# Transposing the residual and the spatial weights on VectorE instead of TensorE in a two-layer decoder trunk

## Chip, cores and metric

The kernel runs on one core of a Trainium2 chip. The metric is the device time of one execution in microseconds; the time of the kernel before is the median of three runs. The profile is of one execution, and times in it count from the start of its span.

## What is computed

A trunk of two layers over 256 positions of width 2048, all in float32. The parts that the change touches are the spatial gate of layer 0 and the residual on its way to the output:

```python
# layer 0: 12 heads g, chunks of 128 positions
w = w_sp * jnp.tril(jnp.ones((CHUNK, CHUNK), w_sp.dtype))
sv = jnp.einsum('gts,bnsgc->bntgc', w, vb) + b_sp.T[None, None, :, :, None]
...
# end of layer 1
x = x + jnp.concatenate([main, mo], axis=-1) @ w_out[l]
x = x + conv_ffn(rmsnorm(x, g_ffn[l]), w_ffn_up[l], conv_w[l], conv_b[l], w_ffn_down[l])
return rmsnorm(x, g_final)
```

The product with `w_sp` sums over s, so TensorE needs each head's 128x128 matrix with s on the partitions, that is, transposed. The residual `x` is kept with features on the partitions (`self.x`, called xT in the profile: 16 blocks of 128 features x 256 positions). The last matrix product and the final norm work with positions on the partitions, so `x` is transposed once into `xt` (two blocks of 128 positions x 2048).

## The kernel before

Nearly all of the work is products of a streamed weight with an activation. Every operand is split in two parts, hi and lo, and each product is made of three matmuls (hi by hi, hi by lo, lo by hi). A weight is read in chunks of 512 KB: `chunk` (L97 on) has SyncE issue the transfer into `raw` (L103; four buffers), ScalarE write the hi part `whi` (L113; four buffers), VectorE write the lo part `wlo` (L114; five buffers), and then TensorE does the chunk's matmuls: `gemm_fm` with the weight as the stationary operand (L152, L153, L155), `gemm_tm` with the activation as the stationary operand (L184 to L186). A product with K = 2048 and 512 output columns is 8 chunks. The engines run as a chain of rings: `raw` of chunk n+4 can be loaded once VectorE has split chunk n, and `whi` of chunk n+4 can be written once TensorE has finished chunk n.

Small tasks are hung between chunks by tables of hooks: `hooks={2: [f]}` runs f in program order after chunk 2. A scheduler then places each instruction in its engine's own order; in places the program order is forced. All of the weight transfers, and the two groups of transfers below, are in the one queue of SyncE, and an engine and that queue each work strictly in order.

The spatial weights: in layer 0, after chunk 5 of the first of three products (`zhooks`, L768), `spatial_load` loads the bias `b_sp` (L755) and `w_sp` (L758, one transfer, tile wsp). During the third product `spatial_turn` (L760) runs after chunks 2, 3 and 4: four TensorE transposes into one PSUM tile (L763), then a VectorE multiplication by the triangular mask `keep` that writes the transposed weights (L765, into the tile slots). They are used some 25 us later. In the same stretch the rotary angles are computed by short VectorE instructions (L350 to L376).

The residual: in layer 1's feed-forward part, the second up-projection of the second group of columns has the hooks `turns` (L1165): after chunks 4 to 7 it runs `turn` (L1110) twice each. A `turn` is four TensorE transposes of 128x128 (L1115) into PSUM and one ScalarE copy to `xt` (L1116). `xt` is first read by `tokens` about 100 us later.

Of the kernel before, what the change touches and what calls it, by code (L numbers as in the profile page):

```python
# [12 lines left out]
AF = mybir.ActivationFunctionType  # L13
ALU = mybir.AluOpType
AX = mybir.AxisListType

P = 128
D = 2048
S = 256
NB = D // P  # L20
GH = 12
GW = GH * 128
# [47 lines left out]
class Kernel:  # L70
# [666 lines left out]
    def layer_a(self):  # L737
        nc, t, tc = self.nc, self.t, self.tc
# [3 lines left out]
        with ExitStack() as ctx:  # L742
# [7 lines left out]
            wT, bb = (wb[:, i * GW : (i + 1) * GW].rearrange("p (g s) -> p g s", g=GH) for i in range(2))  # L750
            spatial = {}


            def spatial_load():
                nc.sync.dma_start(out=bb, in_=t["b_sp"][0].rearrange("(o g) t -> o g t", o=1).to_broadcast([P, GH, P]))  # L755
                raw = self.ap.tile([P, NB * 512], F32, tag="big", name=self.uid("wsp"))
                spatial["raw"] = raw[:, :GW].rearrange("p (g s) -> p g s", g=GH)
                nc.sync.dma_start(out=spatial["raw"], in_=t["w_sp"][0].rearrange("g t s -> t g s"))  # L758

            def spatial_turn(g):  # L760
                acc = self.psum()
                for i in range(4):
                    nc.tensor.transpose(acc[:, i * P : (i + 1) * P], spatial["raw"][:, g + i, :], self.ident)  # L763
                k3 = self.keep.rearrange("p (g s) -> p g s", g=1).to_broadcast([P, 4, P])
                nc.vector.tensor_tensor(wT[:, g : g + 4, :], acc.rearrange("p (g s) -> p g s", g=4), k3, ALU.mult)  # L765

            turns = {2 + i: [lambda i=i: spatial_turn(4 * i)] for i in range(3)}
            zhooks = ({2: [lambda: self.rope_angles(la)], 5: [spatial_load]}, {4: [self.rope_tables]}, turns)  # L768
            for c in range(3):
# [33 lines left out]
            p, parts = {}, {}  # L803
# [287 lines left out]
    def run(self):  # L1091
        nc, tc, t = self.nc, self.tc, self.t
        self.constants()
        with tc.tile_pool(name="mk", bufs=1) as self.mk:
            self.start()
            self.layer_a()
        self.ffn(0, lambda j: self.next_operand(j, None))
        self.layer_b()
        with tc.tile_pool(name="fin", bufs=1) as fin:

            xt = fin.tile([P, 2, D], F32, name="xt")
            gb = fin.tile([P, D], F32, name="gb")
            sums = fin.tile([P, 2, 5], F32, name="fsums")
            part = fin.tile([P, 2], F32, name="fpart")
            r = fin.tile([P, 2], F32, name="froot")
            q = fin.tile([P, 2], F32, name="fq")
            v = fin.tile([P, 2], F32, name="fv")
            nc.sync.dma_start(out=gb, in_=t["g_final"].rearrange("(o d) -> o d", o=1).to_broadcast([P, D]))

            def turn(j):  # L1110
                acc = self.psum()
                for tb in range(2):
                    for i in range(2):
                        o = (2 * tb + i) * P
                        nc.tensor.transpose(acc[:, o : o + P], self.x[:, j + i, tb * P : (tb + 1) * P], self.ident)  # L1115
                nc.scalar.activation(xt[:, :, j * P : (j + 2) * P], acc.rearrange("p (a c) -> p a c", a=2), AF.Copy)  # L1116


            def tokens(j, tb, acc, last, half=None):
                c0, n = (0, 512) if half is None else (256 * half, 256)  # L1120
                c = slice(j * 512 + c0, j * 512 + c0 + n)
                o = xt[:, tb, c]
                add = lambda o, a: nc.vector.tensor_tensor(o, a, o, ALU.add)
                add(o, acc[:, c0 : c0 + n])
                if not last:
                    return
                junk = self.tmp(fin, [P, 512], "fjunk", 2)
                one = lambda x: x[:, tb : tb + 1]
                if half == 1:

                    nc.vector.tensor_tensor_reduce(
                        out=junk[:, :n], in0=o, in1=o, scale=-0.5 / D, scalar=one(part), op0=ALU.mult, op1=ALU.add, accum_out=one(v)
                    )
                else:
                    nc.scalar.activation(junk[:, :n], o, AF.Square, accum_out=sums[:, tb, j : j + 1])
                if half == 0:
                    add(xt[:, tb, j * 512 + 256 : (j + 1) * 512], acc[:, 256:])
                if j < 3:
                    nc.vector.tensor_tensor(o, o, gb[:, c], ALU.mult)
                if j == 2:  # L1140

                    nc.vector.tensor_reduce(one(part), sums[:, tb, 0:3], AX.X, ALU.add)
                    nc.vector.tensor_scalar(one(part), one(part), -0.5 / D, -0.5 * EPS, ALU.mult, ALU.add)
                    nc.scalar.activation(one(r), one(part), AF.Sqrt, scale=-2.0)
                if j == 3:
                    if half != 1:
                        total = one(part) if half == 0 else one(v)
                        nc.vector.tensor_scalar(total, sums[:, tb, 3:4], -0.5 / D, one(part), ALU.mult, ALU.add)
                    if half == 0:
                        return  # L1150

                    nc.scalar.activation(one(r), one(v), AF.Sqrt, scale=-2.0)
                    nc.vector.reciprocal(one(r), one(r))
                    nc.vector.scalar_tensor_tensor(one(q), one(r), one(r), one(v), ALU.mult, ALU.mult)
                    nc.vector.scalar_tensor_tensor(one(r), one(q), 1.5, one(r), ALU.add, ALU.mult)

                    y, rows = xt[:, tb, :], slice(tb * P, (tb + 1) * P)
                    for a in (0, 1024):
                        nc.scalar.activation(y[:, a : a + 512], y[:, a : a + 512], AF.Copy, scale=one(r))
                    nc.vector.tensor_scalar(y[:, 512:1024], y[:, 512:1024], one(r), None, ALU.mult)  # L1160
                    nc.vector.scalar_tensor_tensor(y[:, 1536:], y[:, 1536:], one(r), gb[:, 1536:], ALU.mult, ALU.mult)
                    nc.sync.dma_start(out=self.out[0, rows, :1024], in_=y[:, :1024])
                    (nc.scalar if tb else nc.sync).dma_start(out=self.out[0, rows, 1024:], in_=y[:, 1024:])

            turns = {4: [lambda: turn(0), lambda: turn(2)], 5: [lambda: turn(4), lambda: turn(6)],  # L1165
                     6: [lambda: turn(8), lambda: turn(10)], 7: [lambda: turn(12), lambda: turn(14)]}
            self.ffn(1, to_tokens=turns, tokens=tokens)


# [24 lines left out]
```

## Time and profile before

| | us |
|---|---|
| median of 3 runs (lowest to highest) | 2059.01 (2058.97 to 2060.08) |
| time of the profiled execution | 2058.79 |
| its span | 2057.0 |
| TensorE busy | 2046.9 |
| VectorE busy | 1396.0 |
| ScalarE busy | 1085.6 |
| mean busy share of the DMA engines in most slices | 0.5 to 0.6 |

The busy times are sums over instructions; matmuls overlap, so a busy TensorE is read together with the distance between the starts of its instructions. In a row of the timeline stand the start, the duration, the engine, the line and operation, output and inputs, and in brackets the idle time before it with what ended that. PE is TensorE, DVE VectorE, ACT ScalarE, POOL GpSimd, SPq the DMA queue of SyncE.

### The profile page before, as it was taken

The numbers are of one execution on the slowest core, as the hardware profiler recorded it, in microseconds if no ns is written. First come the engines' busy times: TensorE is split into PE (matmuls) and PEld (weight loads), VectorE is DVE, ScalarE is ACT, GpSimd is POOL, SyncE is SP. The second block draws the span as 40 slices with busy tenths as digits, with TensorE's granted clock in tenths as the row PEclk, the third lists the DMA queues.
The fourth block names the chain that finished last, engine by engine and source line by source line (L and its number), as shares of the span: only waits on it lengthen the run. The fifth ranks groups of instructions, "written<-read, shape, count | busy, mean of one in ns | idle before, by whom it ended". The sixth has DMA issues, their size and how long they took to land.

```text
span 2057.0 us, 39914 instructions
## 1 busy us (share of the span) xinstructions
PE 2046.9 (100%) x16348; PEld 1979.9 (96%) x16348; DVE 1396.0 (68%) x2113; ACT 1085.6 (53%) x1588; POOL 142.0 (7%) x200
## 2 busy tenths in 40 slices
PE   9999999999999999999999999999999999999998
PEld 8989999999999999999999999999988999889996
DVE  6656766777656766457788786776765667646765
ACT  7754744555434555345555575455544555435554
POOL 0000013100000000000043241300000000000000
PEclk9999999999999999999999999999999999999999
DMA  8565555566556665566655635565655666556654
GB/s 288 188 217 176 160 193 198 190 195 195 195 195 195 193 193 193 194 193 194 195 195 176 187 118 178 187 204 177 193 193 194 196 195 195 187 193 195 197 181 154
DMA packets 207692, 392.58 MB, mean 191 GB/s; under 512 B 14158, under 2 KB 23188, under 8 KB 207380
## 3 DMA queue, kind: packets, MB, share of 16 engines
q1 hardware_dynamic: 207316, 389.48, 58.5%
q8 instruction: 128, 2.10, 0.4%
q10 hardware_dynamic: 192, 0.54, 0.1%
q14 instruction: 56, 0.46, 0.1%
HBM read 387.88 MB, written 2.10 MB: 190 GB/s over the span
## 4 chain that ended last, share of the span: by engine, by line
PE 99%; ACT 0%; DVE 0%; DMA 0%; issue 0%; ACTq 0%
PE ps L152 26%; PE ps L153 26%; PE ps L155 26%; PE ps L185 6%; PE ps L184 6%; PE ps L186 6%; PE ps L507 1%; PE ps L400 0%; PE ps L583 0%; PE ps L584 0%; PE ps L582 0%; PE ps L1001 0%; PE ps L790 0%; PE ps L1115 0%; PE ps L1029 0%; DMA graw<-in_g_mem 0%
## 5 line engine op out<-in xcount | busy, mean ns | idle before, releaser
L114 DVE TENSOR_TENSOR wlo<-raw,whi 128x1024 fp32r<-128x1024 f32 x660 | 818.4, 1243 | 531.1 <-ACT whi L113 525.0
L113 ACT ACTIVATE whi<-raw 128x1024 fp32r<-128x1024 f32 x660 | 700.6, 1062 | 857.8 <-PE ps L153 632.3
L152 PE MATMUL ps<-xhl,whi 128*128 128x256 f32 x3264 | 763.2, 277 | 0.0
L153 PE MATMUL ps<-xhl,whi 128*128 128x256 f32 x3264 | 761.2, 276 | 0.0
L153 PEld LDWEIGHTS ps<-xhl,whi 128*128 128x128 f32 x3264 | 612.9, 188 | 0.3
L152 PEld LDWEIGHTS ps<-xhl,whi 128*128 128x128 f32 x3264 | 612.7, 188 | 0.3
L155 PE MATMUL ps<-xhl,wlo 128*128 128x256 f32 x3264 | 436.7, 276 | 0.0
L155 PEld LDWEIGHTS ps<-xhl,wlo 128*128 128x128 f32 x3264 | 400.5, 188 | 0.0
L152 PE MATMUL ps<-h,whi 128*128 128x256 f32 x704 | 163.6, 276 | 0.0
L153 PE MATMUL ps<-h,whi 128*128 128x256 f32 x704 | 163.6, 276 | 0.0
L185 PE MATMUL ps<-wlo,h 128*128 128x512 f32 x354 | 137.2, 388 | 0.0
L184 PE MATMUL ps<-whi,h 128*128 128x512 f32 x354 | 136.8, 388 | 0.0
L186 PE MATMUL ps<-whi,h 128*128 128x512 f32 x354 | 136.8, 388 | 0.0
L153 PEld LDWEIGHTS ps<-h,whi 128*128 128x128 f32 x704 | 132.0, 188 | 0.0
L152 PEld LDWEIGHTS ps<-h,whi 128*128 128x128 f32 x704 | 131.8, 188 | 0.0
L152 PE MATMUL ps<-mainhl,whi 128*128 128x256 f32 x512 | 119.6, 277 | 0.0
L153 PE MATMUL ps<-mainhl,whi 128*128 128x256 f32 x512 | 119.3, 276 | 0.0
L694 ACT ACTIVATE c<-a,cT 128x256 f32<-128x256 f32 x176 | 99.4, 588 | 0.0
L153 PEld LDWEIGHTS ps<-mainhl,whi 128*128 128x128 f32 x512 | 96.0, 188 | 0.0
L152 PEld LDWEIGHTS ps<-mainhl,whi 128*128 128x128 f32 x512 | 95.9, 188 | 0.0
L155 PE MATMUL ps<-h,wlo 128*128 128x256 f32 x704 | 94.1, 276 | 0.0
L232 DVE TENSOR_TENSOR a<-ps,rbc 128x256 f32<-128x256 f32 x176 | 70.0, 418 | 27.6 <-PE ps L155 27.6
(321 smaller groups left out, 2258.6 us busy)
## 6 DMA issues: line engine op xcount, KB each, us to landing
raw<-in_w_ffn_up SPq DMA_DIRECT2D x352, 512.0 KB, 3.5
raw<-in_w_ffn_down SPq DMA_DIRECT2D x176, 512.0 KB, 3.9
raw<-in_w_out SPq DMA_DIRECT2D x64, 512.0 KB, 4.2
raw<-in_w_in_a SPq DMA_DIRECT2D x56, 512.0 KB, 4.3
raw<-in_w_mem_kv SPq DMA_DIRECT2D x31, 512.0 KB, 4.9
raw<-in_w_in_b SPq DMA_DIRECT2D x16, 512.0 KB, 4.6
raw<-in_w_kv_a SPq DMA_DIRECT2D x9, 512.0 KB, 3.6
raw<-in_w_uq SPq DMA_DIRECT2D x12, 384.0 KB, 3.8
```

Source lines behind the costliest of these rows:

```text
L113: nc.scalar.activation(hi[:, :n], raw[:, :n], AF.Copy)
L114: nc.vector.tensor_tensor(lo[:, :n], raw[:, :n], hi[:, :n].bitcast(F32), ALU.subtract)
L152: mm(acc[:, :S], wh, x[:, :S], start=first, stop=False)
L153: mm(acc[:, :S], wh, x[:, S:], start=False, stop=False)
L155: mm(acc[:, :S], wl, x[:, :S], start=False, stop=last)
L184: mm(acc, xh, wh, start=first, stop=False)
L185: mm(acc, xh, wl, start=False, stop=False)
L186: mm(acc, xl, wh, start=False, stop=last)
L232: self.nc.vector.tensor_tensor(out, acc[:, :S], r, ALU.mult)
L507: nc.tensor.matmul(acc[:, :S], w[:, o : o + P], x, start=k == 0 and n == 0, stop=k == NB - 1 and n == 2)
L694: nc.scalar.activation(c, a, AF.Identity, scale=w(2), bias=w(3))
```

## The change

Spatial weights: `w_sp` is loaded by four transfers, one for each 32 columns (s) of the matrices, each into 32 partitions. Each moves 32x48 pieces of 32 floats (128 bytes), so that the 32x32 blocks lie where they must lie after the transpose, each still untransposed. `spatial_turn` then makes one VectorE transpose of 128x512, which turns every 32x32 block in place of its own, and multiplies by the mask from SBUF to SBUF. The TensorE transposes and their PSUM tile are gone.

Residual: `turn(r)` makes one VectorE transpose of 128x1024 (all blocks of 32 positions number r, for r = 0 to 3, of both halves of the positions) into a tile `xs` (two buffers), with its place among VectorE's instructions held in program order, and four transfers on SyncE from 32 partitions to 32 partitions, 1024 pieces of 128 bytes each, which put the blocks in `xt`. The hooks are after chunks 0, 2, 4 and 6. The TensorE transposes and the ScalarE copies are gone.

```diff
-                nc.sync.dma_start(out=spatial["raw"], in_=t["w_sp"][0].rearrange("g t s -> t g s"))
+                blocks = t["w_sp"][0].rearrange("g (m i) (q j) -> q i g m j", i=32, j=32)
+                for q in range(4):
+                    o = raw[32 * q : 32 * (q + 1), :GW].rearrange("i (b j) -> i b j", j=32)
+                    nc.sync.dma_start(out=o, in_=blocks[q].rearrange("i g m j -> i (g m) j"))
 
             def spatial_turn(g):
-                acc = self.psum()
-                for i in range(4):
-                    nc.tensor.transpose(acc[:, i * P : (i + 1) * P], spatial["raw"][:, g + i, :], self.ident)
+                w4 = wT[:, g : g + 4, :]
                 k3 = self.keep.rearrange("p (g s) -> p g s", g=1).to_broadcast([P, 4, P])
-                nc.vector.tensor_tensor(wT[:, g : g + 4, :], acc.rearrange("p (g s) -> p g s", g=4), k3, ALU.mult)
+                nc.vector.transpose(out=w4, in_=spatial["raw"][:, g : g + 4, :])
+                nc.vector.tensor_tensor(w4, w4, k3, ALU.mult)
...
-            def turn(j):
-                acc = self.psum()
-                for tb in range(2):
-                    for i in range(2):
-                        o = (2 * tb + i) * P
-                        nc.tensor.transpose(acc[:, o : o + P], self.x[:, j + i, tb * P : (tb + 1) * P], self.ident)
-                nc.scalar.activation(xt[:, :, j * P : (j + 2) * P], acc.rearrange("p (a c) -> p a c", a=2), AF.Copy)
-
+            def turn(r):
+                xs = self.tmp(fin, [P, 2, NB, 32], "xs", 2)
+                ins = nc.vector.transpose(out=xs, in_=self.x.rearrange("p k (a r j) -> p a k r j", a=2, j=32)[:, :, :, r, :])
+                tc.keep_in_program_order(ins)
+                o = xt[32 * r : 32 * (r + 1)].rearrange("j a (k q i) -> j q (a k) i", q=4, i=32)
+                for q in range(4):
+                    nc.sync.dma_start(out=o[:, q], in_=xs[32 * q : 32 * (q + 1)].rearrange("j a k i -> j (a k) i"))
...
-            turns = {4: [lambda: turn(0), lambda: turn(2)], 5: [lambda: turn(4), lambda: turn(6)],
-                     6: [lambda: turn(8), lambda: turn(10)], 7: [lambda: turn(12), lambda: turn(14)]}
+            turns = {2 * r: [lambda r=r: turn(r)] for r in range(4)}
```

The scheduler moves instructions along with it. VectorE in layer 0, before: chunks 5 and 6 of the first product are split one behind the other (`wlo_1426`, `wlo_1447`), then come the rotary angles.

```order
L350 CAST pos_f<-pos_i 2x128
L114 TENSOR_TENSOR wlo_1426<-raw_1424,whi_1425 128x1024
L114 TENSOR_TENSOR wlo_1447<-raw_1445,whi_1446 128x1024
L354 COPY pos<-ps_1316 128x2
L360 TENSOR_SCALAR ang<-inv,pos 128x32 x2
```

And now, where chunk 5 is `wlo_1426`, chunk 6 `wlo_1450` and chunk 7 `wlo_1468`:

```order
L350 CAST pos_f<-pos_i 2x128
L114 TENSOR_TENSOR wlo_1426<-raw_1424,whi_1425 128x1024
L766 STREAM_TRANSPOSE slots_1255<-wsp_1443 128x512 x3
L114 TENSOR_TENSOR wlo_1450<-raw_1448,whi_1449 128x1024
L354 COPY pos<-ps_1316 128x2
L767 TENSOR_TENSOR slots_1255<-slots_1255,keep 128x512 x3
L114 TENSOR_TENSOR wlo_1468<-raw_1466,whi_1467 128x1024
```

All three transposes and masks have moved from the third product to the first, ahead of the splits of chunks 6 and 7, and the first of the transposes needs all four transfers of `w_sp`. On SyncE two of these stand ahead of the transfers of the positions and the bias, and two behind them; the weight transfers of chunk 7 and on follow. TensorE, whose order moves with it, at the start of chunk 7 (`whi_1467`, `wlo_1468`) of the first product:

```order
L186 MATMUL ps_1257<-whi_1449,xhl_81 128x512
L184 MATMUL ps_1256<-whi_1467,xhl_81 128x512
L184 MATMUL ps_1257<-whi_1467,xhl_81 128x512
L184 MATMUL ps_1488<-whi_1491,xhl_80 128x512
L185 MATMUL ps_1256<-wlo_1468,xhl_81 128x512
```

Before, one L184 stood ahead of a chunk's first L185, which is the first to read `wlo`; now there are three here, and two in chunk 6. The last place is SyncE's queue at the residual's turns. Before it held weight transfers alone; now (the numbers 17368 to 17530 are chunks 1 to 6 of the product with the hooks):

```order
L103 DMA raw_17368<-in_w_ffn_up 128x2x512
L103 DMA raw_17398<-in_w_ffn_up 128x2x512
L103 DMA raw_17434<-in_w_ffn_up 128x2x512
L103 DMA raw_17464<-in_w_ffn_up 128x2x512
L1118 DMA xt<-xs_17362 32x32x32 x4
L103 DMA raw_17500<-in_w_ffn_up 128x2x512
L103 DMA raw_17530<-in_w_ffn_up 128x2x512
L1118 DMA xt<-xs_17428 32x32x32 x4
```

Four transfers of a turn stand behind the weights of chunk 4, and from there four behind every two weights. On VectorE the four transposes (L1114) stand right behind the splits of chunks 0, 2, 4 and 6 of this product.

## The prediction

> **What bounds the kernel.** I read the page's busy shares and chain first, then the two groups that feed TensorE.
>
> ```profile
> PE 2046.9 (100%) x16348; PEld 1979.9 (96%) x16348; DVE 1396.0 (68%) x2113; ACT 1085.6 (53%) x1588; POOL 142.0 (7%) x200
> ...
> PE 99%; ACT 0%; DVE 0%; DMA 0%; issue 0%; ACTq 0%
> ...
> L114 DVE TENSOR_TENSOR wlo<-raw,whi 128x1024 fp32r<-128x1024 f32 x660 | 818.4, 1243 | 531.1 <-ACT whi L113 525.0
> L113 ACT ACTIVATE whi<-raw 128x1024 fp32r<-128x1024 f32 x660 | 700.6, 1062 | 857.8 <-PE ps L153 632.3 <-PE ps L186 149.1 <-issue 34.1
> ```
>
> TensorE is the bound from end to end: 99% of the chain. ScalarE waits for TensorE (857.8 us idle, nearly all released by it), VectorE waits for ScalarE. So the split engines sit at the front of a full ring, and a TensorE instruction that disappears is time saved, while one that is added on VectorE or in the DMA queue costs nothing until the ring has run empty. The question is whether it runs empty.
>
> **What goes from TensorE.** First the chain around the residual's turns, then ScalarE in the same place, whose hi splits are released by the end of each chunk.
>
> ```profile
> 1402.28 0.91 PE ps L155 x8
> 1405.00 0.91 PE ps L155 x8
> 1405.91 0.87 PE ps L1115 x8
> ...
> 1408.63 0.91 PE ps L155 x8
> 1409.55 0.87 PE ps L1115 x8
> ```
>
> ```profile
> 1402.32 1.06 ACT L113 ACTIVATE whi<-raw 128x1024 fp32r<-128x1024 f32 x1 [1.35 <-PE ps L153]
> 1405.04 1.06 ACT L113 ACTIVATE whi<-raw 128x1024 fp32r<-128x1024 f32 x1 [1.66 <-PE ps L153]
> ...
> 1408.67 1.07 ACT L113 ACTIVATE whi<-raw 128x1024 fp32r<-128x1024 f32 x1 [1.20 <-PE ps L153]
> ...
> 1415.91 1.07 ACT L113 ACTIVATE whi<-raw 128x1024 fp32r<-128x1024 f32 x1 [1.18 <-PE ps L153]
> ```
>
> A chunk without transposes takes 2.72 us (1402.32 to 1405.04). With eight transposes it takes (1415.91 - 1405.04) / 3 = 3.62 us. The eight are on the chain and cost 0.90 us; four such chunks make 3.61 us. The spatial turn, on TensorE:
>
> ```profile
> 156.17 0.39 PE L185 MATMUL ps<-wlo,xhl 128*128 128x512 f32 x1
> 156.40 0.39 PE L186 MATMUL ps<-whi,xhl 128*128 128x512 f32 x1
> 156.63 0.60 PE L763 MATMUL ps<-ident,wsp 128*128 128x128 f32 x4
> 156.99 0.48 PE L184 MATMUL ps<-whi,xhl 128*128 128x512 f32 x1
> 157.30 0.40 PE L185 MATMUL ps<-wlo,xhl 128*128 128x512 f32 x1
> ```
>
> From the L186 to the next L185 are 0.90 us; two steps of 0.23 us would be 0.45, so four transposes cost 0.45 us, three turns 1.34 us. In all **4.95 us** leave TensorE. ScalarE's eight copies go too, but ScalarE waits for TensorE there, so they are counted at nothing. This is the gain if nothing that is added comes through.
>
> **What a 128-byte piece costs.** No transfer before has pieces this small, and none goes from SBUF to SBUF. The nearest is the 64 columns of the rotary key weight (L128: 2048 pieces of 256 bytes, nothing else in the queue); beside it stand the stretch of the residual's turns, with pieces of 2 KB, and the two windows in which the spatial weights and the bias are moved before.
>
> ```profile
> 1105.90:1108.40 2.50, 2.50 (x24) 2.50 (x24) 1.68 (x3) 1.24 (x2) 0.65 (x1) 1.00 0.97 210
> ...
> 1380.00:1440.00 60.00, 60.00 (x532) 60.00 (x531) 39.20 (x61) 33.91 (x48) 0.00 (x0) 1.00 0.58 183
> ...
> 106.40:109.00 2.60, 2.60 (x13) 2.17 (x12) 1.66 (x2) 1.06 (x1) 0.00 (x0) 1.00 1.15 331
> 109.00:111.40 2.40, 2.40 (x12) 1.97 (x12) 1.12 (x3) 1.06 (x1) 0.00 (x0) 1.00 1.02 385
> ```
>
> The last two columns are the busy share of the 16 DMA engines and GB/s. In 2.50 us at 210 GB/s the whole 525 KB of the key went through, at a share of 0.97: 0.97 x 16 x 2.50 / 2048 = 18.9 ns of one engine for a piece of 256 bytes. In the 60 us, 183 GB/s are 5360 pieces of 2 KB at a share of 0.58, so 104 ns each. By bytes alone a 128-byte piece would be half of 18.9, 9.5 ns; if a piece has a floor that the 256-byte one is already at, 18.9 ns. The line through the two measured sizes gives 12.8 ns, and I take that, p = 12.8 (9.5 to 18.9).
>
> **Spatial weights: does VectorE starve TensorE?** SyncE's issues, VectorE and ScalarE around them, and the first matmul of the product:
>
> ```profile
> 104.23 0.37 SPq L758 DMA_DIRECT2D wsp<-in_w_sp  x1
> ...
> 105.30 0.35 SPq L755 DMA_DIRECT2D slots<-in_b_sp  x1
> ```
>
> ```profile
> 109.89 0.21 DVE L350 CAST pos_f<-pos_i 2x128 f32<-2x128 int32 x1 [0.60 <-DMA wsp<-in_w_sp]
> 110.79 1.23 DVE L114 TENSOR_TENSOR wlo<-raw,whi 128x1024 fp32r<-128x1024 f32 x1 [0.68 <-ACT whi L113]
> 113.51 1.23 DVE L114 TENSOR_TENSOR wlo<-raw,whi 128x1024 fp32r<-128x1024 f32 x1 [1.50 <-ACT whi L113]
> 114.65 0.15 DVE L354 COPY pos<-ps 128x2 f32<-128x2 f32 x1
> ```
>
> ```profile
> 104.03 0.40 PE L184 MATMUL ps<-whi,xhl 128*128 128x512 f32 x1
> ```
>
> ```profile
> L1139 DVE TENSOR_TENSOR xt<-xt,gb x6: 682/684/686, 2005.6 to 2035.4; 128x512 f32<-128x512 f32 x6
> ...
> L1160 DVE TENSOR_SCALAR xt<-xt,froot x2: 485/486/487, 2046.1 to 2051.3; 128x512 f32<-128x512 f32 x2
> ```
>
> Before, wsp had landed at 109.9, and its 786 KB take 2.4 us at 331 GB/s. Now its 6144 pieces are 384 on each engine, 384 x 12.8 ns = 4.9 us (3.6 to 7.3), and the bias, 786 KB at 385 GB/s or 2.0 us, goes ahead of the last two transfers. It lands at 109.9 + 4.9 - 2.4 + 2.0 = 114.4 (113.1 to 116.8). VectorE is done with chunk 5 at 112.0 and waits there: that is the added wait, and behind it stand the splits of chunks 6 and 7 and the rotary angles. A transpose of 128x512 from SBUF to SBUF has no row; of one source it is 0.49 us in L1160, of two 0.68 in L1139. I take 0.65. Then chunk 6 is split 3 x 0.65 + 1.23 = 3.2 us after the landing, at 117.6 (at most 120.0). A copy of 0.15, three masks of 0.68 and the split of chunk 7 make 3.4 us more: 121.0 (119.7 to 123.4).
>
> TensorE began chunk 0 at 104.03. It begins chunk 6 at 104.03 + 6 x 2.72 = 120.35 and chunk 7 at 123.07, and its new order puts two and three L184 of 0.23 us ahead of the first use of wlo: needed at 120.8 and 123.75. Nothing is late, by 2.7 us, and by 0.35 at the upper end. The cover goes at p = 19.9; each ns beyond costs 0.38 us.
>
> The Trainium skill (VectorE: DVE Perf Modes, The three transpose paths) gives 311 ns for a 128x128 transpose on VectorE in bf16. By it, as an estimate, a 128x512 one takes 1.24 us, and the split of chunk 7 ends at 122.8, still in time; no row here shows one.
>
> **Residual: does the DMA queue starve it?** Four turns bring 16384 pieces, 1024 p = 13.1 us (9.7 to 19.4) on every engine, in batches two chunks (5.44 us) apart. The queue's share for weights is 0.58, so between two batches it has 0.42 x 5.44 = 2.3 us to spare. The weight behind the fourth batch is late by 13.1 - 3 x 2.3 = 6.2 us (2.8 to 12.5). What that may be:
>
> ```profile
> raw<-in_w_ffn_up SPq DMA_DIRECT2D x352, 512.0 KB, 3.5
> ```
>
> Let chunk n-4 end on TensorE at E. ScalarE (1.06) and VectorE (1.23) then split chunk n by E + 2.3, the weight of chunk n+4 is issued and lands 3.5 later, at E + 5.8. TensorE begins chunk n+4 at E + 7 x 2.72 = E + 19.0, so with the two splits it may land at E + 16.7: 10.9 us of cover. So no wait at 12.8 ns; at 18.9 ns one of 1.6 us. The cover goes at p = 17.4, and each ns beyond costs 1.02 us. VectorE's four transposes of 128x1024, about 1.24 us each like L114, are 5.0 us in a stretch in which it is busy 39.2 of 60 us; each delays a split by 1.2 us, which the same ring covers.
>
> **Sum.** 2058.79 of the profiled execution less 4.95 is 2053.8; the median of the runs shown is 0.2 higher, so I predict 2054.0. The ends: at 9.5 ns the same; at 18.9 ns 1.6 us later, 2055.6.
>
> **Rivals.**
> - *Some of it comes back.* p between 18 and 24.5 ns: the waits above are 1.02 (p - 17.4) + 0.38 (p - 19.9), and equal the saving at p = 21.6. At 20 ns 2056.7; at 24.5 ns 2063.1. For it: 18.9 ns was measured at 256 bytes, and SBUF as a source is untested. Against: it needs a smaller piece to be dearer than a larger.
> - *Small pieces cost double, slower.* If each piece under some size took two passes of the engine, p = 25.6, the residual's turns would wait 8.4 us and the spatial ones 2.2 us: 10.6 - 4.95 = 5.6 us slower, 2064.6. It decides from 21.6 ns. Against it: a 256-byte piece by bytes alone is 104 / 8 = 13.0 ns, and 18.9 is no doubling.
> - *VectorE's transpose is slow.*
>
> ```profile
> L257 DVE RECIPROCAL rbr<-rbr 128x256 f32<-128x256 f32 x5 | 8.8, 1753 | 2.5 <-ACT rbr L256 2.5
> ```
>
> At the rate of the slowest row, 6.85 ns a column, 128x512 takes 3.5 us and 128x1024 7.0. The split of chunk 6 ends at 114.4 + 10.5 + 1.2 = 126.1, 5.3 us late, and 28 us of transposes in the 21.8 us of eight chunks, where VectorE has 7.6 idle and the ring some 5.9 of cover, cost 14.5: about 2074. Nothing says that it is this slow.
> - *It doesn't do what it says.* If something else paced the chunks with transposes, their end would not move: 2059. The chain, and ScalarE's waits for TensorE in those very chunks, speak against it.
>
> The Trainium skill (DMA: Bandwidth & Descriptors, Specifications) says that under 512 bytes an engine reads, modifies and writes; that is the second rival's mechanism, and by it 2064.6. The 256-byte row above does not bear it out.
>
> **How the numbers follow.** Forecast 0.66; some comes back 0.13, nearly all within 0.2% of before; doubled pieces 0.10; slow transpose 0.04; no effect 0.07. A measurement of this kernel tells about 0.2%, 4.1 us, from no change, so the forecast counts as faster: 0.66 faster, 0.20 same, 0.14 slower. The range reaches from 2052.8, the spread of the runs (1.1 us) under the sum, to 2062, which takes in the first rival nearly whole and no effect, and leaves out the two slower ones.
>
> **What would show it.** Right: no L763 or L1115; chunks at 2.72 us through both places; the first L766 starting near 114 after a VectorE wait of 2 to 3 us on wsp; TensorE without a gap from 115 to 130 and in the turns. The transfers of a turn taking 3.3 us of a full queue show p. Wrong: a TensorE wait for wlo in chunk 6 or 7, or in the chunks after the fourth turn, or ScalarE waiting for raw there.

## The result, and the profile after

| | before | after |
|---|---|---|
| median of the runs (lowest to highest), us | 2058.94 (2058.52 to 2060.08), 12 runs | 2054.24 (2052.82 to 2055.96), 12 runs |
| profiled execution, us | 2058.79 | 2053.87 |
| its span, us | 2057.0 | 2052.2 |

The ratio is 0.9976, with a 95% interval from 0.9967 to 0.9985: faster by 0.24%, 4.7 us. The forecast was 2054.0.

**The page after: busy times, the chain by engine, and the two groups that feed TensorE.**

```profile
PE 2042.1 (100%) x16304; PEld 1975.3 (96%) x16304; DVE 1401.0 (68%) x2120; ACT 1083.3 (53%) x1581; POOL 142.1 (7%) x200
...
PE 99%; ACT 0%; DVE 0%; DMA 0%; issue 0%; ACTq 0%
...
L114 DVE TENSOR_TENSOR wlo<-raw,whi 128x1024 fp32r<-128x1024 f32 x660 | 818.5, 1243 | 521.9 <-ACT whi L113 516.1
L113 ACT ACTIVATE whi<-raw 128x1024 fp32r<-128x1024 f32 x660 | 700.5, 1062 | 851.7 <-PE ps L153 616.9
```

TensorE has 44 instructions fewer (12 spatial and 32 residual transposes) and is busy 4.8 us less; the span is 4.8 us shorter. VectorE is busy 5.0 us more, and the chain is still TensorE's to 99%, with no line of the change in it. So what was added is hidden.

**Where the time came from.** Every matmul of the kernel before is still there, so its start can be compared between the two traces. This table has the start of the same TensorE instruction after, less before, each counted from the first instruction, as steps in four stretches (the profiled execution of each kernel; the other rows are the experiments below):

| kernel | first 12 us | spatial turns | residual's turns | all else | last matmul |
|---|---|---|---|---|---|
| after | +0.24 | -1.45 | -3.61 | 0.0 | -4.82 |
| residual's part alone | -0.46 | 0.0 | -3.61 | 0.0 | -4.07 |
| spatial part alone | -0.72 | -1.45 | 0.0 | 0.0 | -2.17 |
| transposes put back on TensorE, unused | +0.99 | -1.45 | 0.0 | 0.0 | -0.48 |
| turns spread over two products | -0.40 | -1.45 | -3.61 | 0.0 | -5.48 |
| turns after chunks 0 to 3 | +0.94 | -1.45 | -3.14 | 0.0 | -3.66 |
| half as many pieces more | +1.04 | -1.45 | +3.15 | 0.0 | +2.75 |
| 4 KB pieces | -0.36 | -1.45 | -3.61 | 0.0 | -5.43 |
| spatial transposes late | +0.44 | -1.45 | -3.61 | 0.0 | -4.64 |
| after, once more | -0.11 | -1.45 | -3.61 | 0.0 | -5.14 |
| both parts moved | -0.34 | -1.45 | -3.61 | 0.0 | -5.41 |

Over 2000 us the two traces agree to 0.03 us outside three places: the first 12 us (transfers at the start, which come out a little differently in every execution), the three spatial turns, and the four chunks that had the residual's transposes. The chain of after shows the last of these: 2.72 us from chunk to chunk, where it was 3.62 before.

```profile
1403.80 0.91 PE ps L155 x8
1406.52 0.91 PE ps L155 x8
1409.24 0.91 PE ps L155 x8
1411.96 0.91 PE ps L155 x8
...
1420.12 0.91 PE ps L155 x8
```

**The spatial weights after.** SyncE's issues, then VectorE (the four rows that matter), then the chain where TensorE uses what VectorE made:

```profile
104.47 1.12 SPq L761 DMA_DIRECT2D wsp<-in_w_sp  x2
105.69 1.85 SPq L348 DMA_DIRECT2D pos_i<-in_positions  x1
107.60 0.39 SPq L755 DMA_DIRECT2D slots<-in_b_sp  x1
108.04 1.60 SPq L761 DMA_DIRECT2D wsp<-in_w_sp  x2
```

```profile
116.22 1.90 DVE L766 STREAM_TRANSPOSE slots<-wsp 128x512 f32<-128x512 f32 x3 [3.96 <-DMA wsp<-in_w_sp]
118.04 1.18 DVE L114 TENSOR_TENSOR wlo<-raw,whi 128x1024 fp32r<-128x1024 f32 x1
...
119.21 1.89 DVE L767 TENSOR_TENSOR slots<-slots,keep 128x512 f32<-128x512 f32 x3
121.01 1.22 DVE L114 TENSOR_TENSOR wlo<-raw,whi 128x1024 fp32r<-128x1024 f32 x1
```

```profile
121.17 0.45 PE ps L184 x2
121.63 0.23 PE ps L185
...
123.89 0.68 PE ps L184 x3
124.57 0.23 PE ps L185
```

The added wait is there: VectorE stands still for 3.96 us until `w_sp` has landed at 116.2. Then three transposes take 1.90 us, chunk 6 is split at 119.2 and first used by the L185 at 121.63; chunk 7 is split at 122.2 and used at 124.57. The one is 2.4 us early and the other 2.3, and the chain has no gap.

**The residual after.** SyncE's four batches, one to each turn, and ScalarE's hi splits of the up-projection's weights behind them:

```profile
1385.63 3.79 SPq L1118 DMA_DIRECT2D xt<-xs  x4
...
1391.55 6.42 SPq L1118 DMA_DIRECT2D xt<-xs  x4
...
1399.82 5.63 SPq L1118 DMA_DIRECT2D xt<-xs  x4
...
1408.34 4.71 SPq L1118 DMA_DIRECT2D xt<-xs  x4
```

```profile
1403.27 1.06 ACT L113 ACTIVATE whi<-raw 128x1024 fp32r<-128x1024 f32 x1 [3.13 <-DMA raw<-in_w_ffn_up]
...
1411.13 1.06 ACT L113 ACTIVATE whi<-raw 128x1024 fp32r<-128x1024 f32 x1 [4.89 <-DMA raw<-in_w_ffn_up]
...
1417.74 1.06 ACT L113 ACTIVATE whi<-raw 128x1024 fp32r<-128x1024 f32 x1 [3.84 <-DMA raw<-in_w_ffn_up]
```

TensorE's first matmuls on the weights of the last two rows (chunks 9 and 11 counted from the product with the hooks), in its timeline:

```profile
1415.42 0.28 PE L152 MATMUL ps<-xhl,whi 128*128 128x256 f32 x1
...
1420.86 0.28 PE L152 MATMUL ps<-xhl,whi 128*128 128x256 f32 x1
```

Before, ScalarE waited for TensorE here; now it waits for weights, up to 4.89 us, since these stand in the queue behind the small pieces. The hi split of chunk 9 ends at 1412.19, 3.2 us ahead of its use, that of chunk 11 at 1418.80, 2.1 us ahead. The ring is drained but not empty.

### The profile page after: what moved, and what is told of

It is laid out like the page before. It is cut to its first block, busy times and chain, and to the rows that moved or that the text cites. A ratio compares the mean times of both kernels' runs of the same rounds, so it can differ in the third digit from the quotient of the medians.

```text
span 2052.2 us, 39853 instructions
## 1 busy us (share of the span) xinstructions
PE 2042.1 (100%) x16304; PEld 1975.3 (96%) x16304; DVE 1401.0 (68%) x2120; ACT 1083.3 (53%) x1581; POOL 142.1 (7%) x200
## 4 chain that ended last, share of the span: by engine, by line
PE 99%; ACT 0%; DVE 0%; DMA 0%; issue 0%; ACTq 0%
PE ps L152 26%; PE ps L153 26%; PE ps L155 26%; PE ps L185 6%; PE ps L184 6%; PE ps L186 6%; PE ps L507 1%; PE ps L400 0%; PE ps L583 0%; PE ps L584 0%; PE ps L582 0%; PE ps L1003 0%; PE ps L792 0%; PE ps L1031 0%; PE ps L625 0%; DMA graw<-in_g_mem 0%
## 5 line engine op out<-in xcount | busy, mean ns | idle before, releaser
L155 PE MATMUL ps<-xhl,wlo 128*128 128x256 f32 x3264 | 436.5, 276 | 0.0
L155 PEld LDWEIGHTS ps<-xhl,wlo 128*128 128x128 f32 x3264 | 400.3, 188 | 0.0
L185 PE MATMUL ps<-wlo,h 128*128 128x512 f32 x354 | 137.2, 388 | 0.0
L184 PE MATMUL ps<-whi,h 128*128 128x512 f32 x354 | 136.8, 388 | 0.0
L155 PE MATMUL ps<-h,wlo 128*128 128x256 f32 x704 | 94.1, 276 | 0.0
```

The lines of the kernel that those rows point to most:

```text
L155: mm(acc[:, :S], wl, x[:, :S], start=False, stop=last)
L184: mm(acc, xh, wh, start=first, stop=False)
L185: mm(acc, xh, wl, start=False, stop=False)
```

## Experiments

Times are medians; before was at 2059.07, 2058.67 and 2059.39 on the chips of the three groups of runs.

### Each part alone

Residual's part alone: the spatial part of the diff undone.

```diff
...
+                    nc.tensor.transpose(acc[:, i * P : (i + 1) * P], spatial["raw"][:, g + i, :], self.ident)
...
-                nc.vector.transpose(out=w4, in_=spatial["raw"][:, g : g + 4, :])
...
```

> The residual's turns alone are changed; the spatial weights are transposed on TensorE as before. Theory (only what leaves TensorE counts, the rest is hidden): 3.6 us under the kernel before (four chunks of 0.90), near 2055.3, ratio 0.9982. Rival (the two parts share one cause, such as the freed PSUM tiles or the scheduler's new order in layer 0): clearly less, within 1.5 us of before. In the profile no chunk longer than 2.72 us around 1400 us, and TensorE without a wait there.

Measured 2054.60 us, ratio 0.9977 (0.9968 to 0.9986). Spatial part alone: the residual's turns put back on TensorE and ScalarE.

```diff
...
-            turns = {2 * r: [lambda r=r: turn(r)] for r in range(4)}
+            turns = {4: [lambda: turn(0), lambda: turn(2)], 5: [lambda: turn(4), lambda: turn(6)],
+                     6: [lambda: turn(8), lambda: turn(10)], 7: [lambda: turn(12), lambda: turn(14)]}
```

> The spatial weights alone are changed. Theory: 1.3 us under the kernel before (three turns of 0.45), near 2057.6, ratio 0.9993, which five rounds may hardly tell from no change; the sum with the residual alone gives the whole change, -4.9. Rival (VectorE's wait for the four transfers comes through to TensorE): no gain or a loss, with a TensorE wait for wlo between 115 and 130 us.

Measured 2057.35 us, ratio 0.9992 (0.9983 to 1.0001); the interval reaches just over 1, so the times alone do not show a gain of the spatial part. The medians give 4.5 and 1.7 us, together more than the 4.7 us of the whole change, since the first 12 us scatter (-0.46 and -0.72 us in the profiled executions). The table separates this: 3.61 and 1.45 us, and each part leaves the other's place untouched. In the table the parts add up.

### TensorE's time put back, nothing else

The 32 transposes run again after chunks 4 to 7, into PSUM tiles that nobody reads; VectorE's transposes and the transfers stay.

```diff
+            def dead(j):
+                acc = self.psum()
...
+                        nc.tensor.transpose(acc[:, o : o + P], self.x[:, j + i, tb * P : (tb + 1) * P], self.ident)
...
+            for n in range(4):
+                turns.setdefault(4 + n, []).extend([lambda n=n: dead(4 * n), lambda n=n: dead(4 * n + 2)])
```

> The changed kernel with the 32 TensorE transposes of the residual put back at their old chunks as dead work: they write PSUM tiles that nobody reads, and no ScalarE copy follows. Theory (it is TensorE's own time that was saved): 3.6 us over the changed kernel, near 2057.9, ratio to before 0.9994. Rival (the gain is ScalarE's eight copies gone, or waits that hung on them): stays within 1 us of the changed kernel, near 2054.5.

Measured 2057.20 us, ratio 0.9991 (0.9982 to 1.0000), 3.0 us over after by the medians. Its chain has the transposes (L1125) where the kernel before had them, 3.62 us from chunk to chunk:

```profile
1404.52 0.91 PE ps L155 x8
1405.43 0.87 PE ps L1125 x8
1408.16 0.91 PE ps L155 x8
1409.07 0.87 PE ps L1125 x8
```

In the table the residual's step goes from -3.61 to 0.0. ScalarE's eight copies are gone in this kernel too, and give nothing. So the gain at the residual is TensorE's own time, to the hundredth; that something else paced those chunks is ruled out. The spatial transposes were not put back in this way; for them the same cause rests on the trace, where the 1.45 us come in three equal steps of 0.48, one at each of the three turns.

### How near the queue is to coming through

Turns after chunks 0 and 4 of two products, so that the pieces have twice the time:

```diff
-                    turns = to_tokens if to_tokens is not None and g == 1 else {}
+                    turns = {} if to_tokens is None else to_tokens.get(g, {})
...
-            turns = {2 * r: [lambda r=r: turn(r)] for r in range(4)}
+            turns = {g: {4 * i: [lambda r=2 * (g - 1) + i: turn(r)] for i in range(2)} for g in (1, 2)}
```

> The residual's four turns stand after chunks 0 and 4 of two products instead of after chunks 0, 2, 4 and 6 of one. Theory (the transfers are hidden as they are, with about 1 us of cover left): the time of the changed kernel within 0.7 us, near 2054, but ScalarE's waits for raw (14.9 us in the changed kernel) almost gone. Rival (in some executions the cover runs out, which would also be why the changed kernel's runs scatter over 3 us): 1 us faster, near 2053.3, and a narrower scatter.

Measured 2053.13 us, ratio 0.9971 (0.9961 to 0.9982). That is 1.1 us under the first median of after, the number of the rival and not of the theory; the last experiment comes back to it. Turns after chunks 0, 1, 2, 3, so that they have half the time:

```diff
-            turns = {2 * r: [lambda r=r: turn(r)] for r in range(4)}
+            turns = {r: [lambda r=r: turn(r)] for r in range(4)}
```

> The four turns stand after chunks 0, 1, 2 and 3, so their transfers come at half the distance. In the changed kernel the DMA engines were busy 30.1 us from 1384 to 1416; less 13.1 us for the weights' 2 KB pieces, 17.0 us fall to 1024 pieces of 128 bytes on each engine, 16.6 ns each. Theory (the ring gives 10.9 us of cover, and no more): the weight behind the last batch is late by 17.0 - 3 x 1.14 = 13.6 us, so TensorE waits some 2.7 us, near 2057. By the predicted 12.8 ns it would be late by 9.7 us and TensorE would not wait: 2054. Rival (transfers of this size are hidden whatever their place): 2054.

Measured 2053.79 us, ratio 0.9977 (0.9968 to 0.9987). ScalarE's waits from 1380 to 1440, first in after and then in the kernel with half the time (columns: us in all, times, longest). With the turns spread there is none in this stretch, but the last batch then begins only at 1439.7; up to 1480 there are two such waits, 3.5 us in all.

```profile
ACT whi L113 <- DMA raw<-in_w_ffn_up: 14.9, 7, 4.9
```

```profile
ACT whi L113 <- DMA raw<-in_w_ffn_up: 10.8, 6, 4.1
```

Spreading takes ScalarE's waits from 14.9 to 3.5 us and changes nothing on TensorE's steps, as it should when the ring covers them. The tight version missed its expectation: TensorE lost 0.47 us by the table, not 2.7, and the time is that of the rival. The 0.47 us are one wait of 0.20 us and 0.27 around it. Undisturbed, these matmuls take 0.28 us and start 0.11 apart, so two of them overlap by 0.16; at the wait that overlap is lost, and the matmul behind it takes 0.39 us, so that the next starts 0.11 later than it would.

```profile
1416.46 0.39 PE L152 MATMUL ps<-xhl,whi 128*128 128x256 f32 x1 [0.20 <-ACT whi L113]
1416.69 0.28 PE L153 MATMUL ps<-xhl,whi 128*128 128x256 f32 x1
```

VectorE's transposes and SyncE's queue say why the loss is so small:

```profile
1385.04 1.24 DVE L1114 STREAM_TRANSPOSE xs<-xT 128x1024 f32<-128x1024 f32 x1
1387.77 1.24 DVE L1114 STREAM_TRANSPOSE xs<-xT 128x1024 f32<-128x1024 f32 x1
1395.54 1.25 DVE L1114 STREAM_TRANSPOSE xs<-xT 128x1024 f32<-128x1024 f32 x1 [4.97 <-DMA xt<-xs]
1401.52 1.24 DVE L1114 STREAM_TRANSPOSE xs<-xT 128x1024 f32<-128x1024 f32 x1
```

```profile
1386.31 4.19 SPq L1118 DMA_DIRECT2D xt<-xs  x4
1390.60 0.75 SPq L103 DMA_DIRECT2D raw<-in_w_ffn_up  x1
1391.44 9.71 SPq L1118 DMA_DIRECT2D xt<-xs  x8
...
1403.49 6.98 SPq L1118 DMA_DIRECT2D xt<-xs  x4
```

The staging tile `xs` has two buffers, so the third transpose waits until the first batch has been moved. That wait throttles the batches: they still take 24 us (1386.3 to 1410.5), three weights went ahead of the last of them, and the load on the queue is hardly denser than in after. My sum had let the batches arrive one chunk (2.72 us) apart. The test did not double what it was to double, so it decides little about the cover.

The next one did: six transfers a turn instead of four, the extra two into a tile that nobody reads.

```diff
+            xd = fin.tile([P, 32, 36], F32, name="xd")
...
+                    if q < 2:
+                        b = 32 * (2 * (r % 2) + q)
+                        nc.sync.dma_start(out=xd[b : b + 32, :, :32], in_=xs[32 * q : 32 * (q + 1)].rearrange("j a k i -> j (a k) i"))
```

> The changed kernel with half as many transfers again in each turn (two of the four are made a second time, into a tile that nobody reads). Theory, at 16.6 ns a piece: 25.5 us of pieces on each engine, late by 25.5 - 6.9 = 18.6 us against 10.9 of cover, so TensorE waits 7.7 us: near 2062, over the kernel before. At 12.8 ns it would wait 1.9: 2056. Rival (the DMA queue does not reach TensorE): 2054.

Measured 2063.25 us, ratio 1.0027 (1.0018 to 1.0037): slower than before. TensorE's timeline (of an execution of 2061.44 us) now has the waits that the prediction said would show it wrong:

```profile
1418.82 0.39 PE L152 MATMUL ps<-xhl,whi 128*128 128x256 f32 x1 [2.43 <-ACT whi L113]
...
1428.31 0.39 PE L152 MATMUL ps<-xhl,whi 128*128 128x256 f32 x1 [2.15 <-ACT whi L113]
```

So the mechanism of the prediction's first rival (some of it comes back) is real and close by: half as many pieces more turn a gain of 3.61 us in this place into a loss of 3.15, 6.76 us apart. The two waits are 4.58 of these. Most of the rest is the granted clock, the column ahead of the last two in this table by window:

```profile
1418.80:1420.00 1.20, 1.18 (x9) 1.18 (x10) 1.20 (x1) 0.00 (x0) 0.00 (x0) 0.88 0.29 28
1420.00:1422.00 2.00, 2.00 (x11) 2.00 (x11) 0.76 (x2) 1.06 (x1) 0.00 (x0) 0.50 0.82 127
1422.00:1424.00 2.00, 2.00 (x15) 2.00 (x14) 1.65 (x5) 1.09 (x2) 0.00 (x0) 0.72 0.99 153
1424.00:1426.00 2.00, 2.00 (x20) 1.97 (x18) 2.00 (x6) 0.37 (x1) 0.00 (x0) 1.00 0.89 257
...
1428.30:1430.00 1.70, 1.69 (x14) 1.69 (x15) 1.70 (x3) 1.70 (x4) 0.00 (x0) 1.00 0.97 363
```

At these shares 0.12 x 1.2 + 0.50 x 2.0 + 0.28 x 2.0 = 1.7 us of TensorE's work are lost. The last 0.5 us are what the tight version lost around its wait as well, 0.27 us for each of the two.

The time came near the 2062 of the expectation, but not as it was added up: 7.7 us of waits were expected and 4.6 came, and the loss of the clock stood in no sum. The median is 1.8 us over the profiled execution and the slowest of the ten took 2067.67 us; nine of the ten list a mean granted clock of 0.997, the profiled one 0.998. So the others may have lost more of the clock, but no trace of one was kept.

### Number of pieces or number of bytes

The same bytes in the same four transfers, but in pieces of 4 KB (the blocks then do not lie where they belong in `xt`):

```diff
-                o = xt[32 * r : 32 * (r + 1)].rearrange("j a (k q i) -> j q (a k) i", q=4, i=32)
+                o = xt[32 * r : 32 * (r + 1)].rearrange("j a (h c) -> j (a h) c", h=2)
...
-                    nc.sync.dma_start(out=o[:, q], in_=xs[32 * q : 32 * (q + 1)].rearrange("j a k i -> j (a k) i"))
+                    nc.sync.dma_start(out=o[:, q], in_=xs[32 * q : 32 * (q + 1)].rearrange("j a k i -> j (a k i)"))
```

> The same transfers from the same places in the queue, with the same bytes, but each partition's 4 KB written as one piece; the blocks are not put where they belong, so the output is not the reference's. Theory (the number of pieces fills the queue, not the bytes and not the place behind VectorE's transpose): ScalarE's waits for raw around the turns, 14.9 us in the changed kernel, are gone, and the time is the changed kernel's, near 2054, as those waits never reached TensorE. Rival (the place in the queue holds the weights back): the waits for raw stay.

Measured 2053.25 us, ratio 0.9973 (0.9963 to 0.9983). ScalarE's waits for weights in the same stretch:

```profile
ACT whi L113 <- DMA raw<-in_w_ffn_up: 4.6, 2, 2.7
```

They fall from 14.9 to 4.6 us, with the bytes and the places in the queue unchanged; they are not gone, as was expected. So it is mostly the number of pieces that holds the weights back; TensorE's timeline is the same.

### The spatial transposes at their hooks

```diff
-                nc.vector.transpose(out=w4, in_=spatial["raw"][:, g : g + 4, :])
+                tc.keep_in_program_order(nc.vector.transpose(out=w4, in_=spatial["raw"][:, g : g + 4, :]))
```

> The spatial transposes and masks on VectorE in program order too, in the third product, when the four transfers have long landed. Theory (VectorE's wait of 4.0 us on them is covered by the ring): the wait is gone and the time is the changed kernel's within 0.7 us, near 2054. Rival (the wait costs TensorE something): up to 2 us faster.

Measured 2053.16 us, ratio 0.9973 (0.9964 to 0.9982). The transposes now run in the third product, from 148.6 to 154.4, and wait for nothing:

```profile
L766 DVE STREAM_TRANSPOSE slots<-wsp x3: 704/706/706, 148.6 to 154.4; 128x512 f32<-128x512 f32 x3
```

VectorE's wait of 3.96 us is gone, and TensorE's step stays at -1.45: the wait cost nothing.

### Is anything left?

Three versions whose TensorE steps equal those of after stood about 1 us under its first median. So after was run once more, beside a kernel with both parts moved (turns spread, spatial transposes at their hooks; both edits are above).

> The changed kernel once more, beside the kernel with both of its parts moved, on one chip. Theory: the 1.0 us between 2054.2 of the changed kernel and the 2053.1 to 2053.3 of the versions with spread turns, big pieces or late spatial transposes is the scatter of the first 12 us, since TensorE's timeline is the same behind them. Then this kernel is at 2053.2 to 2054.3, and within 0.7 us of the one with both parts moved. Rival: those versions are truly 1 us faster; then this kernel is at 2054.2 or above and the other at 2053.1 or below, at least 1 us apart.

Measured 2053.91 us (2053.24 to 2055.02), ratio 0.9974 (0.9964 to 0.9985).

> Both parts moved: the residual's turns after chunks 0 and 4 of two products instead of 0, 2, 4, 6 of one, and the spatial transposes at their hooks in the third product. TensorE's instructions are the same in number as in the changed kernel. Theory (TensorE never waits in either): within 0.7 us of the changed kernel on the same chip, 2053.2 to 2054.3, ratio to before near 0.9975, and less waiting of ScalarE for weights in the up-projection (about 4 us instead of 15). Rival (waits that the trace does not show cost about 1 us): at least 1 us faster than the changed kernel, 2053.1 or below.

Measured 2053.33 us (2053.07 to 2054.62), ratio 0.9973 (0.9962 to 0.9983). They are 0.58 us apart, within the 0.7 of the theory, and their runs overlap, though seven of the eight with both parts moved lie under 2053.6 and three of the other eight. In the profiled executions nearly the whole difference (0.23 of 0.27 us at the last matmul) lies in the first 12 us. Less that column of the table, the six profiled executions with the steps -1.45 and -3.61 take 2053.62 to 2053.67 us. So a few tenths between the medians may be real, but in the traces they do not come from the turns; why the starts would differ stays open. The versions are not shown to be faster than the change. What speaks for spreading the turns is the margin, not the time.

## Why the prediction was right

- **What goes from TensorE** (3.61 + 1.34 = 4.95): right. The residual's turns gave 3.61, the spatial ones 1.45 (0.48 for a turn instead of 0.45). The chain's spacing before (3.62 against 2.72) was the whole of the larger term, and the kernel with the transposes put back shows that no other cause is needed. 5.06 less 0.24 in the first 12 us is the 4.82 of the profiled execution. The two sizes below that were off, the price of a piece and the landing of wsp, entered the forecast only as waits of nothing; that 2054.24 lies so near 2054.0 says nothing for them.
- **p, a 128-byte piece, 12.8 ns (9.5 to 18.9)**: too low as it acts in the queue. This window of after covers the four batches:

```profile
1384.00:1416.00 32.00, 32.00 (x285) 32.00 (x284) 22.13 (x29) 14.36 (x18) 0.00 (x0) 1.00 0.94 195
```

  An engine is busy 0.94 x 32 = 30.1 us. Of the 6.24 MB, 2.10 are the residual's; the other 4.14 MB are 126 pieces of 2 KB to an engine, 13.1 us at the 104 ns of before. The rest, 17.0 us over 1024 pieces, is 16.6 ns. This charges everything else in the queue to the pieces. The trace's records of the single pieces give 15.5 ns in the mean for these 16384 and 13.0 at the median, and 109 in the mean for the 2 KB pieces beside them. So 12.8 ns was right for the typical piece; what it missed is the dearer mean in a full queue. By the prediction's sum the last weight is then 17.0 - 6.9 = 10.1 us late. It landed at 1417.7, and was wanted at 1420.86 - 2.3 = 1418.6: 0.9 of the 10.9 us are left, so it was 10.0 late, as 16.6 ns says and not the 6.2 of 12.8 ns. The cover held, and by this sum p = 17.4, where it goes, is only 0.8 ns away. But a lo split may end a little into the chunk (L155, the first to read it, comes last in it), so the true margin is larger: the 2.1 us seen above, or 2.0 ns a piece.
- **wsp lands at 114.4 (113.1 to 116.8)**: 116.2, near the upper end. Between its first issue and then, the engines did this:

```profile
104.40:116.20 11.80, 11.80 (x53) 9.51 (x52) 3.89 (x4) 4.82 (x5) 1.12 (x32) 1.00 1.18 213
```

  1.18 x 11.8 = 13.9 us of an engine (records overlap, so the share passes 1). 2.51 MB less the 0.79 of wsp are 53 pieces of 2 KB to an engine, 5.5 us; the other 8.4 us over 384 pieces would make 22 ns. The records of the single pieces give 19.6 ns in the mean and 13.0 at the median; the rest went into the other pieces in the queue, 125 ns in the mean for 2 KB and 337 for the bias's 6 KB, where before they took 101 and 254. So these pieces, read from HBM, were dearer in the mean than the residual's, read from SBUF, but not at the median; no run separates the source from what else was in the queue. SyncE's rows add to it: the transfers of the positions and of the bias, between the two pairs, were issued 0.7 and 2.3 us later than before. The landing was 1.8 us late, but the chunks themselves began 0.8 us later than my 120.35 and 123.07, and VectorE's way from the landing to the split of chunk 7 took 6.0 us for my 6.6. So the margin came out at 2.3 us for 2.7, by errors against each other; that part is luck.
- **L766, 0.65 us**, and **L1114, about 1.24 us** (behind the count: shortest, median and longest in ns):

```profile
L766 DVE STREAM_TRANSPOSE slots<-wsp x3: 670/671/711, 116.2 to 117.4; 128x512 f32<-128x512 f32 x3
...
L1114 DVE STREAM_TRANSPOSE xs<-xT x4: 1240/1241/1245, 1384.4 to 1402.1; 128x1024 f32<-128x1024 f32 x4
```

  Right: in this kernel a 32x32-block transpose costs VectorE what an elementwise pass over the same tile costs (0.67 us beside the mask's 0.69 for 128x512, 1.24 beside the split's 1.24 for 128x1024). The Trainium skill (VectorE: DVE Perf Modes, The three transpose paths) led to an estimate of 1.24 us for 128x512; the trace has 0.67, about half.
- **What would show it**: one of the signs named for wrong did come. ScalarE waited for raw behind the turns, 14.9 us in all, and TensorE did not wait. The sign was badly chosen: it shows a ring that drains, not one that is empty. A wait that the prediction did not count came too: VectorE's fourth transpose stood 1.3 us until one of the two xs buffers was free.
- **Some comes back (0.13)**: not here, but its mechanism was shown by the kernel with half as many pieces more, which is slower than before.
- **Small pieces cost double (0.10)**: no. 16.6 ns for 128 bytes in the mixed queue is not above the 18.9 of 256 bytes, and even the pieces of wsp, at 19.6 ns in the mean, stay under the 25.6 of this rival. The medians of the single pieces settle it: 13 ns at 128 bytes, 18 at 256, 27 at 512, 46 at 1 KB, 65 at 1.5 KB and 84 at 2 KB. The line through 512 bytes and 2 KB gives 12.8 at 128 and 17.5 at 256, so there is no step at 512. The rule of the Trainium skill that I had set beside it (DMA: Bandwidth & Descriptors, Specifications, read-modify-write under 512 bytes) is not borne out as a doubled price; the part of it that no run shows is what an engine does inside.
- **Slow transpose, no effect**: no, by L1114 and by the transposes put back.

## What to carry to other kernels

Where one engine is the chain from end to end, the spacing of its instructions with and without the work to be removed gives the gain (here 3.61 us for 3.61 and 1.45 for 1.34); the uncertainty lies in whether what is added stays under the ring's cover. Work out that cover as a time, then the price per piece at which it goes, and size an added transfer by its number of pieces as well as by its bytes: here about 2 ns a piece lay between the full gain and the first wait, and in the experiment half as many pieces again lay between a gain and a loss. When the cover is that thin, spread the pieces, even though it shows no gain.

## What the runs showed of the hardware that was not expected

- **A short TensorE wait costs more than itself.** With half as many pieces more, the granted clock fell to 0.50 behind a wait of 2.43 us: by the shares in the rows above from 1419.7 to 1423.1, that is 0.9 us after TensorE had begun again and for 3.4 us. Behind the wait of 2.15 us it stayed at 1.00. The Trainium skill (TensorE: Matmul & The Clock Gate, Part 1) puts the fall to half rate behind an idle window of about 3.4 us; here 2.43 us of the 3.4 before the fall were idle, and that was enough. It is one wait of each kind, so no threshold follows.
- **The price of a piece is a fixed part and a part by bytes.** The medians of the single pieces in after lie within 1 ns of 8 ns + 0.037 ns a byte from 128 bytes to 2 KB; at 128 bytes it is 13 ns for those from HBM and those from SBUF alike. The means are higher where the queue is full: 13.5 to 15.5 ns for the residual's pieces, 18.3 to 19.9 for those of wsp.
- **A transfer of many pieces holds its queue at the issue.** SyncE took 3.8 to 6.4 us to issue a turn's four transfers (9.71 for eight in the tight version), but 2.4 to 2.8 us for the same four in 4 KB pieces, and 0.37 us for one weight transfer in an open queue. So weights behind many pieces are not only served but also issued late.
- **The scatter between the profiled executions sits at the start.** Over eleven profiled executions the first 12 us differ from those of before by -0.72 to +1.04 us; the rest of the timeline, some 2030 us, repeats to 0.03 us where no engine waits anew.
